# A phase's first two down weights split ahead of its last evacuation, and the last pair's silu queued behind them on ScalarE

## The chip, the cores and the metric

The kernel runs on one core of one Trainium2 chip. The time is device microseconds of one execution; the lower the better. A core has TensorE (matmuls, and the loads of their stationary operands, which the profile lists as PEld), VectorE (DVE), ScalarE (ACT), GpSimd (POOL) and SyncE (SP, used here to issue transfers). Each engine works through its own queue in order; semaphores connect them.

## The reference, cut to what matters

One layer of a hybrid encoder on 512 tokens of width 1024, in float32. The change lies in the last part, the channel mixer with its gated convolution:

```
h = rms_norm(x, norm_ffn_g)
up = causal_dwconv(h @ w_up, conv_ffn_w)     # 1024 -> 2 x 2816, three taps along the tokens
a, b = split(up, 2)
x = x + (silu(a) * b) @ w_down               # 2816 -> 1024
out = rms_norm(x, norm_f_g)
```

## The kernel before, in words

**Precision.** Every float32 operand of a matmul is split into a rounded half `h` and a remainder `l`, and a product is three matmuls: wh·xh, wl·xh and wh·xl. For a weight this is the work of `split()`: ScalarE copies the raw weight into `wh` (line 274), VectorE subtracts it to get `wl` (line 278). Both tiles have two buffers, so a weight can be split only once TensorE has finished with the weight two before it in the stream.

**Stream.** All weights stand in one list, `stream`, in the order in which they are used; `raws` counts those being loaded, `parts` those already split. `split()` also issues the raw loads some places ahead, on SP's queue.

**Phases.** The 22 pairs (a, b) of 128 hidden columns are done in two phases, pairs 0 to 11 and 12 to 21. In a phase the up products of its pairs come first: `up()` runs two blocks of matmuls per pair (`p_up`, one for a and one for b), and evacuates each: VectorE multiplies the sums by the norm factor (`fz`, line 1155), `taps` applies the three-tap convolution (ScalarE line 565, VectorE lines 566 and 569, result `fu`). After the second block `glu()` forms silu(a) on ScalarE (line 1215) and a·b: on GpSimd for most pairs, for a phase's last pair on VectorE and later (line 1232). Two pairs make a quadrant q, from which `glu` derives the forms that the fast matrix product needs: sums and differences (`t13`, `t24`, lines 1237 to 1242) and their halves `gh`, `gl` (`hl`, lines 1246 and 1247).

Then come the phase's down steps, in `seven()`: a fast product of 2 × 2 blocks with seven multiplications, whose weights come in two chunks per step, named P (three forms) and F (four forms). The first step of phase 0 uses P18 and F18, that of phase 1 P30 and F30. `seven()` takes a chunk, runs its matmuls (`passes`, line 326; for each chunk first all matmuls with `wh`, then those with `wl`), and then splits the next chunk by `split_next()` if that has not been done. In phase 1 the chunks are P30, F30, P31, F31 and so on; quadrant 10, of the last two pairs, is first needed by P33, in the fourth step. In phase 0 quadrant 5, of its last two pairs, is first needed by the fifth step.

**Order.** Where work is not to run at once, it is put into the list `later` as (due chunk, cost in us, tags, function). After each split `run_later` runs what is due within a budget that depends on the kind of chunk (for an F 0.75, for a P 1.6, for an up weight 1.7, or 4.2 while entries tagged `("e",)` wait). `flush` and `flush_only` run entries with given tags at once. The tag `("e",)` marks the evacuation of the pairs 1, 2 and 5, whose up products are also done by `seven()` (`merge`), and of up blocks evacuated while such entries still wait. Everything run from `later` is traced under `after_split()`, so on ScalarE it is queued behind the last `wh` traced so far, and on VectorE behind the last `wl`. `glu()` sets the due chunks of its follow-up work from the number of chunks split at that moment (k = len(parts) − 1): for a phase's last pair the product at k + 3, the sums at k + 4, the halves at k + 5 and k + 6. It also runs at once what is left of earlier quadrants.

Outside these rules the framework's scheduler orders each engine's queue from the order of tracing and from what it takes to be ready.

**The place of the change.** In `up()`, for the last pair of a phase (j = 11 and j = 21) and its second block (i = 1), after the block's matmuls are traced, `split_next()` splits the first P chunk. If entries tagged `("e",)` wait, they are flushed and one more chunk is split. Then the block is evacuated and `glu()` is called.

Of the kernel before, what the change touches and what calls it, by code (L numbers as in the profile page):

```python
# [10 lines left out]
AF = mybir.ActivationFunctionType  # L11
# [31 lines left out]
PHASES = ((0, 12), (12, NP))  # L43
# [27 lines left out]
def block_kernel(ctx, tc, xT, vecs, wv, win, wmix, wo, wup, wst, wdp, outT):  # L71
# [3 lines left out]
    nc = tc.nc  # L75
# [6 lines left out]
    def keep(ins):  # L82
        return tc.keep_in_program_order(ins)
# [70 lines left out]
    raws, parts, order = [], [], {}  # L154
    pools = {"raw": wp}
    later = []
    held = dict.fromkeys(NRAW, 0)

    def after_split():

        st = ExitStack()
        for ins in order.values():
            st.enter_context(tc.issue_after(ins))
        return st

    def tag_of(k):
        return "raw" if stream[k][0][0] != "F" else "rf" if k >= ff0 else "rg"

    def load(upto):
        for k in range(len(raws), min(upto, len(stream) - 1) + 1):  # L170
            nm, src, ncol = stream[k]
            tag = tag_of(k)
            if held[tag] == NRAW[tag] or tag not in pools:
                return
            held[tag] += 1
            raw = pools[tag].tile([P, D], F32, tag=tag, name=f"raw_{nm}", bufs=NRAW[tag])
            if k == 0:

                keep(nc.scalar.dma_start(raw[:, VB:ncol], src[:, VB:]))
                keep(nc.sync.dma_start(raw[:, :VB], src[:, :VB]))  # L180
            else:
                keep(nc.sync.dma_start(raw[:, :ncol], src if tag == "raw" else made[src]))
            raws.append(raw[:, :ncol])
# [39 lines left out]
    def run_later(k, us):  # L223

        n = 0
        while n < len(later):
            if later[n][0] <= k and later[n][1] <= us + 0.1:
                us -= later[n][1]
                with after_split():
                    later.pop(n)[3]()  # L230
            elif later[n][0] <= k:
                return
            else:
                n += 1
# [11 lines left out]
    def flush_only(tags):  # L246

        while n := [n for n, w in enumerate(later) if set(w[2]) & set(tags)]:
            with after_split():
                later.pop(n[0])[3]()  # L250

    def split(hl=None):

        k = len(parts)
        if k == len(stream):
            return
        nm, _, ncol = stream[k]
        load(k + (LOOK if len(raws) > KB else AHEAD))
        if hl is None:
            hl = []  # L260
            for x in "hl":
                if k == 0:
                    wp.tile([P, PADW[x]], F32, tag=f"pad{x}", name=f"pad_{x}")
                w0 = VOFF if k < KB else 0
                hl.append(wp.tile([P, D], F32R, tag=f"w{x}", name=f"w{x}_{nm}", bufs=2)[:, w0 : w0 + ncol])
        hi, lo = hl
        raw = raws[k]
        if k == 0:
            for cs in (slice(VB, S + H), slice(0, VB)):
                keep(nc.vector.tensor_copy(hi[:, cs], raw[:, cs]))  # L270
        elif k == 1:
            keep(nc.vector.tensor_copy(hi, raw))
        else:
            ins = nc.scalar.activation(hi, raw, AF.Copy)  # L274
            order["hi"] = ins.ins
            if k < KB:
                keep(ins)
        ins = nc.vector.tensor_sub(lo, raw, hi.bitcast(F32))  # L278
        order["lo"] = ins.ins
        if k < KB:  # L280
            keep(ins)
        held[tag_of(k)] -= 1
        parts.append((hi, lo))
        if any(("e",) in w[2] for w in later):
            run_later(k, {"u": 4.2, "P": 1.6, "F": 1.2}[nm[0]])
            return
        run_later(k, {"u": 1.7, "P": 1.6, "F": 0.75, "i": 3.0, "m": 3.0, "d": 0 if nm == "dp1" else 2.1}.get(nm[0], 3.5))
# [275 lines left out]
    def taps(u, z, w):  # L563

        nc.scalar.activation(u, z, AF.Copy, scale=col(w + 2))
        nc.vector.scalar_tensor_tensor(  # L566
            u[:, 1:], z[:, : S - 1], col(w + 1), u[:, 1:], op0=ALU.mult, op1=ALU.add
        )
        nc.vector.scalar_tensor_tensor(  # L569
            u[:, 2:], z[:, : S - 2], col(w), u[:, 2:], op0=ALU.mult, op1=ALU.add  # L570
        )
# [117 lines left out]
    z, e, o = (ap.tile([n, S], F32, tag="pp", name=nm, bufs=NPP) for nm in ("fz", "fe", "fo"))  # L689
# [104 lines left out]
    for i in range(n + LA):  # L794
# [8 lines left out]
        if 0 <= i - LA < n:  # L803
            pr, e, qb = units[i - LA]
# [151 lines left out]
    for j in range(KB):  # L956
# [26 lines left out]
        a, b = gs  # L983
# [141 lines left out]
    def up(j, ph, rb2, pu=None):  # L1125
        uu = []

        def tap(i, z):
            u = fp.tile([P, S], F32, tag="fu", name=f"fu{j}{i}", bufs=3)
            taps(u, z, CF + 3 * (2 * j + i))  # L1130
            uu.append(u)

        if j in SUP:
            c = len(GATES) + 2 * SUP.index(j)
            slot()
            seven(
                UPD[c - len(GATES) :][:2], c, {j: USETS[j]}, up_form, of="x",
                done=lambda i, banks, ids: merge(ph, j, banks, ids, rb2, tap, uu),
            )
            slot()  # L1140
            return
        evacs = []
        for i in range(2):
            slot()
            p = pu[i] if pu else block(f"up{2 * j + i}", x1h, x1l, True)
            if i and j + 1 == PHASES[ph][1]:
                split_next()
                if any(("e",) in w[2] for w in later):
                    flush_only((("e",),))
                    split()  # L1150
            z = [None]

            def mul(i=i, p=p, z=z):
                z[0] = fp.tile([P, S], F32, tag="fz", name=f"fz{j}{i}", bufs=4)
                nc.vector.tensor_mul(z[0], p, rb2)

            evac = [(0.7, mul), (1.4, lambda i=i, z=z: tap(i, z[0]))]
            if i:
                evac.append((0, lambda: glu(ph, j, uu)))
            if any(("e",) in w[2] for w in later):  # L1160
                later.extend((0, us, (("e",), acc.last) if x == 0 else (("e",),), f) for x, (us, f) in enumerate(evac))
            else:
                for _, f in evac:
                    f()
# [46 lines left out]
    def glu(ph, j, uu):  # L1211
        a, b = uu
        q, k = j // 2, len(parts) - 1
        g0 = place(ph, q)
        nc.scalar.activation(a, a, AF.Silu)
        if j == NP - 1:
            nc.scalar.activation(tbl, a[: 4 * H, :1], AF.Sqrt, scale=0.0, bias=eps[: 4 * H])
        if j % 2 == 0:
            ge = glu.even = fp.tile([P, 2, 2 * P], F32, tag="ge", name=f"ge{q}", bufs=2)
            keep(nc.gpsimd.tensor_mul(ge, a.rearrange(halves_of, h=2), b.rearrange(halves_of, h=2)))  # L1220
            return
        flush_only([("q", x) for x in range(q)])
        ge = glu.even
        go = fp.tile([P, 6, 2 * P], F32, tag="gr", name=f"go{q}")

        def mul(eng):
            return eng.tensor_mul(go[:, 0:2, :], a.rearrange(halves_of, h=2), b.rearrange(halves_of, h=2))

        if j + 1 < PHASES[ph][1]:
            keep(mul(nc.gpsimd))  # L1230
        else:
            later.append((k + 3, 0.7, (("q", q),), lambda: mul(nc.vector)))
        b11, b12 = ge[:, 0, :], ge[:, 1, :]
        b21, b22, t1, t2, t3, t4 = (go[:, i, :] for i in range(6))

        def t13():
            nc.vector.tensor_sub(t1, b11, b12)
            nc.vector.tensor_sub(t3, b22, b12)

        def t24():  # L1240
            nc.vector.scalar_tensor_tensor(t2, t1, -1.0, b22, op0=ALU.mult, op1=ALU.subtract)
            nc.vector.scalar_tensor_tensor(t4, t2, -1.0, b21, op0=ALU.mult, op1=ALU.subtract)

        def hl(src, gs):
            def f():
                nc.scalar.activation(gh[:, gs, :], src, AF.Copy)
                nc.vector.tensor_sub(gl[:, gs, :], src, gh.bitcast(F32)[:, gs, :])

            return f


        d = (2, 3, 4) if j + 1 < PHASES[ph][1] else (4, 5, 6)
        w = [(d[0], 0.85, t13), (d[0], 0.85, t24), (d[1], 0.7, hl(ge[:, : 1 + ph, :], slice(g0, g0 + 1 + NF * ph, NF)))]
        w += [(d[x > 0 and 2 or 1], 0.7, hl(go[:, x : x + 2, :], slice(g0 + 1 + x, g0 + 3 + x))) for x in (0, 4, 2)]
        at = next((x for x, i in enumerate(later) if ("e",) in i[2]), len(later))
        later[at:at] = [(k + n, us, (("q", q),), f) for n, us, f in w]
# [265 lines left out]
```

## Time and profile before

| | us |
|---|---|
| median of 3 runs | 695.1 |
| lowest and highest | 694.63, 695.14 |
| profiled execution, its own time | 695.06 |
| its span, first to last instruction | 693.2 |
| TensorE busy | 685.2 |
| VectorE busy | 537.2 |
| ScalarE busy | 359.9 |
| GpSimd busy | 178.5 |

The mean granted clock of TensorE is 0.997 of full speed. Phase 0's down steps begin near 466 us of the span, phase 1's near 633 us. In a timeline row the columns are start (us from the start of the span), duration in us, engine, line of the kernel, operation, output and inputs by name, shapes, and, in brackets, how long the engine had been idle before it and what released it. In a row of a stretch the columns are its bounds, its length, then the busy time and the number of instructions of TensorE, of the weight loads, of VectorE, ScalarE and GpSimd, then the granted clock, the share of the transfer engines that was busy, and GB/s.

### The profile page before, as it was taken

To read this page: it belongs to the slowest core of one execution; us is meant where nothing else is said; L and a number is where in the kernel's file an instruction comes from. 1 tells how busy PE (TensorE), PEld (TensorE's weight loads), DVE (VectorE), ACT (ScalarE), POOL (GpSimd) and SP (SyncE) were. 2 spreads that over 40 slices of the span, in tenths; PEclk is the share of its full clock that TensorE was granted. 3 is DMA by queue.
4 is the path that set the end of the run, shared out by engine and by line. 5 is a ranking of instruction groups with operands and counts; after the bars stand their busy time and mean duration, and the time that the engine had idled before them with its cause. 6 is when DMAs were issued, how large, how long until landed. Compare 5 with 4: busy or idle time off the path is not lost.

```text
span 693.2 us, 14638 instructions
## 1 busy us (share of the span) xinstructions
PE 685.2 (99%) x5960; PEld 683.7 (99%) x5960; DVE 537.2 (77%) x833; ACT 359.9 (52%) x568; POOL 178.5 (26%) x195
## 2 busy tenths in 40 slices
PE   9999999999999999999999999999999999999996
PEld 9999999999999999999999999999999999999996
DVE  6677887877578778869778699998774677877794
ACT  5575755555554444446554555545443344445572
POOL 6124947542020201214400143320000313222000
PEclk9999999999999999999999999999999999999998
DMA  8628999553568586787887486585647686766513
GB/s 311 218 66 290 217 238 213 132 124 92 183 145 220 165 272 200 232 306 158 126 279 240 125 190 175 143 219 193 192 132 227 143 194 159 185 171 178 156 31 122
DMA packets 60019, 127.57 MB, mean 184 GB/s; under 512 B 5376, under 2 KB 27920, under 8 KB 59696
## 3 DMA queue, kind: packets, MB, share of 16 engines
q1 hardware_dynamic: 41880, 101.51, 44.5%
q0 software_dynamic: 16832, 23.93, 22.0%
q10 hardware_dynamic: 1240, 1.19, 0.5%
q8 instruction: 47, 0.77, 0.5%
q14 instruction: 20, 0.16, 0.1%
HBM read 124.45 MB, written 41.42 MB: 239 GB/s over the span
## 4 chain that ended last, share of the span: by engine, by line
PE 89%; DVE 9%; issue 1%; ACT 1%; DVEq 0%; ACTq 0%
PE dn L326 25%; PE p_up L308 16%; PE p_in L308 14%; PE p_wo L308 6%; PE p_up L326 5%; PE yc L308 3%; PE ya L308 3%; DVE wl_up L278 2%; DVE fu L566 2%; PE pa L476 2%; PE pb L478 2%; PE p_q L308 2%; PE p_k L308 2%; PE o L657 2%; PE tp L640 1%; DVE fu L569 1%
## 5 line engine op out<-in xcount | busy, mean ns | idle before, releaser
L308 PE MATMUL p_up<-x1h,wh_up 128*128 128x256 f32 x464 | 90.4, 276 | 0.0
L308 PE MATMUL p_up<-x1h,wl_up 128*128 128x256 f32 x464 | 90.4, 276 | 0.0
L308 PE MATMUL p_up<-x1l,wh_up 128*128 128x256 f32 x464 | 90.3, 276 | 0.0
L210 POOL DMA_DIRECT2D f<-in_wst_dram x60 | 70.9, 1316 | 0.3 <-issue 0.2
L308 PEld LDWEIGHTS p_up<-x1h,wl_up 128*128 128x128 f32 x464 | 69.9, 188 | 0.0
L308 PEld LDWEIGHTS p_up<-x1l,wh_up 128*128 128x128 f32 x464 | 69.8, 188 | 0.0
L308 PEld LDWEIGHTS p_up<-x1h,wh_up 128*128 128x128 f32 x464 | 69.8, 188 | 0.0
L274 ACT ACTIVATE wh_up<-raw_up 128x1024 fp32r<-128x1024 f32 x38 | 40.2, 1057 | 53.4 <-PE p_up L308 42.9
L278 DVE TENSOR_TENSOR wl_F<-raw_F,wh_F 128x1024 fp32r<-128x1024 f32 (+1 forms) x38 | 51.0, 1343 | 17.9 <-ACT wh_F L274 17.9
L274 ACT ACTIVATE wh_F<-raw_F 128x1024 fp32r<-128x1024 f32 (+1 forms) x38 | 40.0, 1053 | 35.9 <-PE dn L326 27.2
L278 DVE TENSOR_TENSOR wl_up<-raw_up,wh_up 128x1024 fp32r<-128x1024 f32 x38 | 48.7, 1282 | 12.0 <-ACT wh_up L274 12.0
L308 PE MATMUL p_in<-xgh,wh_in 128*128 128x256 f32 x288 | 56.8, 279 | 0.0
L308 PE MATMUL p_in<-xgh,wl_in 128*128 128x256 f32 x288 | 56.6, 278 | 0.0
L308 PE MATMUL p_in<-xgl,wh_in 128*128 128x256 f32 x288 | 56.5, 278 | 0.0
L1220 POOL TENSOR_TENSOR ge<-fu,fu 128x512 f32<-128x512 f32 x11 | 16.7, 1520 | 146.9 <-DVE fu L569 116.1
L274 ACT ACTIVATE wh_P<-raw_P 128x768 fp32r<-128x768 f32 (+1 forms) x38 | 31.7, 834 | 32.9 <-PE dn L326 23.8
L278 DVE TENSOR_TENSOR wl_P<-raw_P,wh_P 128x768 fp32r<-128x768 f32 (+1 forms) x38 | 36.6, 962 | 15.4 <-ACT wh_P L274 9.5
L326 PE MATMUL dn<-gh,wh_F 128*128 128x256 f32 x192 | 45.2, 277 | 0.7 <-ACT wh_F L274 0.7
L308 PEld LDWEIGHTS p_in<-xgh,wh_in 128*128 128x128 f32 x288 | 44.7, 188 | 0.7
L326 PE MATMUL dn<-gl,wh_F 128*128 128x256 f32 x192 | 45.1, 276 | 0.0
L308 PEld LDWEIGHTS p_in<-xgl,wh_in 128*128 128x128 f32 x288 | 43.7, 188 | 0.0
L308 PEld LDWEIGHTS p_in<-xgh,wl_in 128*128 128x128 f32 x288 | 43.6, 188 | 0.0
(343 smaller groups left out, 2150.7 us busy)
## 6 DMA issues: line engine op xcount, KB each, us to landing
raw_up<-in_wup_dram SPq DMA_DIRECT2D x38, 512.0 KB, 5.1
raw_F<-f SPq DMA_DIRECT2D x37, 512.0 KB, 5.3
raw_P<-in_wst_dram SPq DMA_DIRECT2D x37, 384.0 KB, 4.8
raw_in<-in_win_dram SPq DMA_DIRECT2D x24, 512.0 KB, 3.8
f<-in_wst_dram POOLq DMA_DIRECT2D x37, 256.0 KB, 6.4
f<-in_wst_dram SPq DMA_DIRECT2D x18, 512.0 KB, 7.0
f<-in_wst_dram POOLq DMA_DIRECT2D x18, 512.0 KB, 7.8
f<-f SPq DMA_DIRECT2D x36, 256.0 KB, 6.2
```

The costliest lines, as they stand in the source:

```text
L210: return lambda: keep(nc.gpsimd.dma_start(dst, src, accum_op=ALU.add))
L274: ins = nc.scalar.activation(hi, raw, AF.Copy)
L278: ins = nc.vector.tensor_sub(lo, raw, hi.bitcast(F32))
L308: keep(nc.tensor.matmul(out[:, cs], w, x[:, cs], start=start and i == 0 and c == 0, stop=stop and i == 2 and c == len(cut) - 1,))
L326: keep(nc.tensor.matmul(out, wl if x == 1 else wh, xl if x == 2 else xh, start=opens and bk not in seen, stop=closes and bk not in left,))
L476: keep(nc.tensor.matmul(pa[t][:, :VW], xt, w[:, VB:], start=start, stop=stop))
L478: keep(nc.tensor.matmul(pb[t], xt, w[:, :VB], start=start and t % 2 == 0, stop=stop and t % 2 == 1))
L566: nc.vector.scalar_tensor_tensor(u[:, 1:], z[:, : S - 1], col(w + 1), u[:, 1:], op0=ALU.mult, op1=ALU.add)
L569: nc.vector.scalar_tensor_tensor(u[:, 2:], z[:, : S - 2], col(w), u[:, 2:], op0=ALU.mult, op1=ALU.add)
L640: keep(nc.tensor.transpose(tp[:, ks], pt[:, ks], ident))
L657: keep(nc.tensor.matmul(o[:, 2 * P * e + c0 : 2 * P * (e + 1)], w, x[:, kb, c0:], start=e == 0 and kb == 0 and i == 0, stop=e == 1 and kb ...
L1220: keep(nc.gpsimd.tensor_mul(ge, a.rearrange(halves_of, h=2), b.rearrange(halves_of, h=2)))
```

## The change

Two places change. In `up()`, at the end of a phase, the second `split()` no longer depends on whether entries tagged `("e",)` wait: the phase's first P chunk and its first F chunk are both split there, and only then are such entries flushed. In `glu()`, for the last pair of a phase, the silu is traced under `issue_after(order["hi"])`, which queues it on ScalarE behind the last `wh` traced so far, here that of the F chunk.

```diff
@@ -1145,9 +1145,8 @@
             p = pu[i] if pu else block(f"up{2 * j + i}", x1h, x1l, True)
             if i and j + 1 == PHASES[ph][1]:
                 split_next()
-                if any(("e",) in w[2] for w in later):
-                    flush_only((("e",),))
-                    split()
+                split()
+                flush_only((("e",),))
             z = [None]
 
             def mul(i=i, p=p, z=z):
@@ -1212,7 +1211,8 @@
         a, b = uu
         q, k = j // 2, len(parts) - 1
         g0 = place(ph, q)
-        nc.scalar.activation(a, a, AF.Silu)
+        with tc.issue_after(order["hi"]) if j + 1 == PHASES[ph][1] else ExitStack():
+            nc.scalar.activation(a, a, AF.Silu)
         if j == NP - 1:
             nc.scalar.activation(tbl, a[: 4 * H, :1], AF.Sqrt, scale=0.0, bias=eps[: 4 * H])
         if j % 2 == 0:
```

## The prediction

> **What bounds the kernel now.** I read the page first, then the waits of the TensorE, then the stretches of the span, and last the timeline at the two places that the diff touches.
>
> ```profile
> span 693.2 us, 14638 instructions
> PE 685.2 (99%) x5960; PEld 683.7 (99%) x5960; DVE 537.2 (77%) x833; ACT 359.9 (52%) x568; POOL 178.5 (26%) x195
> ```
> ```profile
> PE warm L115 <- DVE ones L107: 1.1, 1, 1.1
> PE dn L326 <- ACT wh_F L274: 0.7, 1, 0.7
> ```
> ```profile
> 397.00:465.00 68.00, 68.00 (x602) 68.00 (x602) 65.63 (x94) 34.89 (x52) 23.71 (x19) 1.00 0.72 186
> 465.00:524.00 59.00, 58.34 (x514) 58.15 (x514) 45.70 (x63) 28.96 (x37) 0.00 (x0) 1.00 0.59 181
> 627.00:669.00 42.00, 42.00 (x370) 41.81 (x370) 34.00 (x49) 24.91 (x34) 3.18 (x3) 1.00 0.46 132
> ```
>
> The matmuls fill the span. TensorE waits for another engine twice, once at the start (the `warm` row) and once, 0.7 us, for a `wh_F`, the rounded half of a down weight made by ScalarE. In the stretches (length, then busy time of PE, weight loads, VectorE, ScalarE, GpSimd, then granted clock) only 465 to 524, where phase 0 goes from up blocks to down steps, has idle PE; the clock is 1.00 in all three. VectorE is 97% busy (65.63 of 68) just before. So this edit can win only that one hole, and can lose by opening others. Phase 0's first down weights are P18 and F18, phase 1's P30 and F30.
>
> ```profile
> 464.01 0.94 DVE L278 TENSOR_TENSOR wl_P<-raw_P,wh_P 128x768 fp32r<-128x768 f32 x1
> 464.12 0.72 ACT L565 ACTIVATE fu<-fz,vec 128x512 f32<-128x512 f32 x1 [2.13 <-DVE fz L1155]
> 464.75 1.66 ACT L1246 ACTIVATE gh<-go 128x512 fp32r<-128x512 f32 x3
> 465.85 0.39 PE L308 MATMUL p_up<-x1l,wh_up 128*128 128x256 f32 x2
> 466.47 0.74 DVE L569 SCALAR_TENSOR_TENSOR fu<-fz,vec,fu 128x510 f32<-128x510 f32 x1
> 467.13 1.28 DVE L1247 TENSOR_TENSOR gl<-go,gh 128x512 fp32r<-128x512 f32 x2
> 467.30 0.63 ACT L1215 ACTIVATE fu<-fu 128x512 f32<-128x512 f32 x1 [0.90 <-DVE fu L569]
> 467.32 0.76 PEld L326 LDWEIGHTS dn<-gh,wl_P 128*128 128x128 f32 x6
> 467.84 1.04 ACT L274 ACTIVATE wh_F<-raw_F 128x1024 fp32r<-128x1024 f32 x1
> 468.33 0.68 DVE L1155 TENSOR_TENSOR fz<-p_up,rb_n 128x512 f32<-128x512 f32 x1
> 468.93 0.19 PEld L326 LDWEIGHTS dn<-gh,wh_F 128*128 128x128 f32 x1 [0.85 <-ACT wh_F L274]
> 469.04 0.19 PEld L326 LDWEIGHTS dn<-gl,wh_F 128*128 128x128 f32 x1
> 470.73 0.94 DVE L278 TENSOR_TENSOR wl_P<-raw_P,wh_P 128x768 fp32r<-128x768 f32 x1
> 471.67 0.19 PEld L326 LDWEIGHTS dn<-gh,wh_P 128*128 128x128 f32 x1
> 473.03 0.75 PEld L326 LDWEIGHTS dn<-gh,wl_P 128*128 128x128 f32 x6
> ```
> The reader sees ScalarE stand for 0.90 us until the last pair's first tap chain (`fu` L569) is done, then take its silu (L1215), and only then `wh_F`. P18's lower-half loads begin at 467.32, F18's first load at 468.93.
>
> ```profile
> 631.08 0.63 ACT L1215 ACTIVATE fu<-fu 128x512 f32<-128x512 f32 x1 [1.92 <-DVE fu L569]
> 631.73 1.28 ACT L1217 ACT_TABLE_LOAD   x1
> 632.71 0.39 PE L308 MATMUL p_up<-x1l,wh_up 128*128 128x256 f32 x2
> 633.02 0.29 ACT L1217 ACTIVATE tbl<-fu,ex 32x1 f32<-32x1 f32 x1
> 633.14 0.69 DVE L1155 TENSOR_TENSOR fz<-p_up,rb_n 128x512 f32<-128x512 f32 x1 [2.15 <-PE p_up L308]
> 633.23 1.04 ACT L274 ACTIVATE wh_F<-raw_F 128x1024 fp32r<-128x1024 f32 x1
> 634.18 0.71 ACT L565 ACTIVATE fu<-fz,vec 128x512 f32<-128x512 f32 x1
> 634.19 0.76 PEld L326 LDWEIGHTS dn<-gh,wl_P 128*128 128x128 f32 x6
> 634.79 0.83 ACT L274 ACTIVATE wh_P<-raw_P 128x768 fp32r<-128x768 f32 x1
> 634.87 0.19 PEld L326 LDWEIGHTS dn<-gh,wh_F 128*128 128x128 f32 x1
> 634.98 0.19 PEld L326 LDWEIGHTS dn<-gl,wh_F 128*128 128x128 f32 x1
> 637.59 0.19 PEld L326 LDWEIGHTS dn<-gh,wh_P 128*128 128x128 f32 x1
> ```
> At the end of phase 1 the same hand-over has no hole: silu, the load of the square-root table and its one small use lie in a ScalarE gap before the up weights' buffer is free.
>
> **The change, part by part.**
> *What really moves.* No instruction is added or taken away; order and due times change. The `("e",)` entries come only from pairs 1, 2 and 5; after pair 5 an up split may spend 4.2 and an evacuation adds 2.1 (the code's own units), so the queue of 6.9 is empty four splits on, long before pair 11, and phase 1 makes none. The moved `flush_only` thus finds nothing, and the old branch, second split included, never ran. New is: F18 and F30 are split, unconditionally, before the last product is evacuated; the silu is queued behind their `wh_F`; and as `glu` counts from the number of split chunks, the last quadrant's follow-up work falls due one chunk later.
>
> *Phase 0, the gain.* `wh_F` reuses the buffer of the last up weight, whose last matmul runs to 465.85 + 0.39 = 466.24, so this is its earliest start; it would end at 467.28. F18's load is wanted one undisturbed step after 467.32. Phase 1 gives that step: from the `wl_P` group to the second F load, 634.98 − 634.19 = 0.79. Here it is 469.04 − 467.32 = 1.72. The hole is worth 0.93 us, more than the 0.7 or 0.85 of the wait rows, because the restart is slow too. With `wh_F` ready at 467.28 against a need at about 468.0, all of it should go: −0.93. From below: 0, if `wh_F` still starts late. I take the full value since ScalarE is free at 464.75 + 1.66 = 466.41 and nothing ahead of `wh_F` then waits.
>
> *Phase 0, what hides the displaced work.* The silu goes from 467.30 to about 467.9 at the earliest; its product is due several chunks on. The two last `gh`/`gl` parts of quadrant 4, which `glu` flushes, get behind F18's halves as well. VectorE holds the same instructions. At 467.2 it has `fz` (its matmul ended at 466.24) or `wl_F` ready, so it need not stand. The next deadline is the second down step's `wl_P`: done at 470.73 + 0.94 = 471.67, needed at 473.03, which comes 0.93 earlier, at 472.10. Cover: 0.43 us. Cost 0; if VectorE stands for longer than 0.43, the excess goes to TensorE.
>
> *Phase 1, the loss.* `wh_F` cannot start before 632.71 + 0.39 = 633.10. Silu, table load and small use leave the gap and stand behind it. ScalarE then runs: `wh_F` from 633.14 (starts 0.95 apart by 633.23 and 634.18), `fu` from 634.09 (0.61 on, by 634.18 and 634.79), silu 634.70 (0.65), table load 635.35 (1.29), small use 636.64 (0.21 to 0.29), second step's `wh_P` from 636.85 to 637.70. Its first load is wanted at 637.59 and starts some 0.05 after the half is made (468.93 against 467.84 + 1.04 in phase 0): a stall of about 0.16, with a slow restart 0.2. Bounds: 0 if the scheduler puts `wh_P` in front, 0.5 if the small use and the restart take twice as long. I take 0.2, which the row sum gives.
>
> [...]
>
> *Phase 1, due times.* Quadrant 10 is consumed in the fourth down step.
> ```profile
> 641.69 0.42 DVE L1241 SCALAR_TENSOR_TENSOR go<-go 128x256 f32<-128x256 f32 x1
> 642.14 0.42 DVE L1242 SCALAR_TENSOR_TENSOR go<-go 128x256 f32<-128x256 f32 x1
> 643.99 0.68 DVE L1247 TENSOR_TENSOR gl<-ge,gh 128x512 fp32r<-128x512 f32 x1
> 644.90 0.96 DVE L278 TENSOR_TENSOR wl_P<-raw_P,wh_P 128x768 fp32r<-128x768 f32 x1 [0.22 <-ACT wh_P L274]
> 645.77 1.89 DVE L1247 TENSOR_TENSOR gl<-go,gh 128x512 fp32r<-128x512 f32 x3
> ```
> ```profile
> 647.22 0.28 PE L326 MATMUL dn<-gh,wh_P 128*128 128x256 f32 x1
> ```
> One chunk later, the split budgets (0.75 for an F, 1.6 for a P) leave the second pair of sums (641.69 to 642.56, 0.87) and the `ge` part (0.6) behind the `wl_P` of 644.90 instead of ahead of it. The three `go` parts then start at 645.77 + 0.87 + 0.6 = 647.24 instead of 645.77; the second, the last this step needs, ends at about 648.50. TensorE reaches it as its twelfth matmul, 647.22 + 11 × 0.114 = 648.47. So the margin is gone: 0.05. Bounds: 0, and 1.2 if the next `wl_F` gets in between. Quadrant 5 in phase 0 has the same lateness with a step more before it is used; cost 0.
>
> *DMA and queues.* `load` runs inside the split, so SP's next raw loads are issued in the same order; each waits for the raw buffer that the `wl` before it frees. GpSimd has nothing in 465 to 524, and nothing of its queue moves. No wait of TensorE names a DMA.
>
> *Sum.* The profiled execution took 695.06 (span 693.2, and 1.86 outside); the median of the runs shown is 695.1, 0.04 above. 695.06 − 0.93 + 0.2 + 0.05 = 694.38, so 694.4.
>
> **Rivals.**
> *The hole only moves (695.2).* ScalarE or VectorE reaches the second step late by what F18 gained: the 0.43 of cover is passed by about 0.9. For it: VectorE's 97% before the hand-over. Against it: the instructions are the same, and one of two is always ready. 694.4 + 0.9 = 695.3; with `wh_F` not earlier at all, 695.06 + 0.25 = 695.3; I give 695.2.
>
> *Slower: VectorE stands at `wl_F`.* If the scheduler queues `wl_F` straight behind the `wl_P` of 464.01, VectorE has nothing to run from 464.95 until `wh_F` is made at 467.28: 2.33 us, of which 1.9 pass the cover. 694.4 + 1.9 = 696.3. From 2.5 us of such standing on it decides: 0.2% of 695.06 is 1.39, which is also about what a measurement of this kernel can tell from no change; with some of the bound of the fourth step it comes to 696.7. Against it: the old order also had `wl_F` behind everything ready, and in phase 1 `fz` went first. [...]
>
> *Faster by more than 1.39.* TensorE has no other hole to close from 397 to 669, so nothing in the trace pays for it: 693.6 at best.
>
> **How the numbers follow.** Forecast (most of 0.93 gained, 0 to 0.6 given back) 0.62, its own range 693.9 to 695.0; hole moved 0.22, at 695.2; VectorE standing 0.12, of which 0.10 lies past 695.06 + 1.39 = 696.45 and 0.02 short of it; more gain 0.04. So faster by over 0.2% has 0.04, slower 0.10, and within 0.2% 0.62 + 0.22 + 0.02 = 0.86. The low end, 693.7, is the whole gain against the fastest run shown, 694.63 − 0.93; the high end, 695.9, takes in the moved hole, the upper bound of the second step's stall, and the near part of the slower case. Left out is about 0.15.
>
> **What would show it.** Right: at about 465 to 470 the PE wait for `wh_F` is gone, silu starts after `wh_F`, and the `wl_P` group and second F load stand 0.8 apart. Phase 1: table load after `wh_F` near 635, a short PE wait for `wh_P` near 637.6 less the gain, the `gl` parts of quadrant 10 behind the fourth step's `wl_P`. Wrong if VectorE shows an idle stretch before `wl_F`, or if TensorE shows a wait of a microsecond at the second or fourth step.

## The result, and the profile after

The changed kernel takes 696.1 us (median of 20 runs, 695.69 to 696.61), the kernel before 695.05 (20 runs, 694.56 to 696.16). The ratio is 1.0015, with a 95% interval of 1.0008 to 1.0022: slower by about 1 us, where 0.7 us less was forecast. The time lies 0.2 above the stated range.

The waits of TensorE, in the changed kernel:

```profile
PE dn L326 <- DVE gl L1247: 1.4, 1, 1.4
PE warm L115 <- DVE ones L107: 1.1, 1, 1.1
```

The same work is in it, from its page:

```profile
PE 685.5 (99%) x5960; PEld 683.9 (99%) x5960; DVE 537.4 (77%) x833; ACT 359.6 (52%) x568; POOL 178.6 (26%) x195
```

The wait for `wh_F` is gone, and one twice as long stands in another place, on another engine. The stretches of the changed kernel tell where (bounds, length, busy time of PE, weight loads, VectorE, ScalarE, GpSimd):

```profile
465.00:524.00 59.00, 58.97 (x520) 58.77 (x520) 45.69 (x64) 29.24 (x37) 0.00 (x0) 1.00 0.58 184
627.00:669.00 42.00, 40.64 (x356) 40.38 (x355) 32.82 (x47) 23.97 (x33) 2.46 (x3) 1.00 0.45 127
```

The hand-over of phase 0 has 58.97 us of matmuls in 59 (58.34 before); the down steps of phase 1 have 40.64 in 42 (42.00 before). First phase 0, from the timeline of the changed kernel:

```profile
466.22 1.06 ACT L274 ACTIVATE wh_F<-raw_F 128x1024 fp32r<-128x1024 f32 x1 [0.96 <-ACT gh L1246]
467.22 0.75 PEld L326 LDWEIGHTS dn<-gh,wl_P 128*128 128x128 f32 x6
468.01 0.19 PEld L326 LDWEIGHTS dn<-gl,wh_F 128*128 128x128 f32 x1
468.43 0.62 ACT L1215 ACTIVATE fu<-fu 128x512 f32<-128x512 f32 x1
470.63 0.73 DVE L569 SCALAR_TENSOR_TENSOR fu<-fz,vec,fu 128x510 f32<-128x510 f32 x1
471.29 0.94 DVE L278 TENSOR_TENSOR wl_P<-raw_P,wh_P 128x768 fp32r<-128x768 f32 x1
472.29 0.77 PEld L326 LDWEIGHTS dn<-gh,wl_P 128*128 128x128 f32 x6 [0.23 <-DVE wl_P L278]
```

`wh_F` starts at 466.22, the silu comes after it, and P18's `wl_P` group and the second F18 load stand 468.01 − 467.22 = 0.79 apart, as in an undisturbed step: the whole 0.93 is won. Of it about 0.3 is lost again at once, since the second step's `wl_P` is late (the weight loads stand 0.23 for it). From the first step's `wl_P` loads to the second's it was 473.03 − 467.32 = 5.71 before and is 472.29 − 467.22 = 5.07 now: a net gain of 0.64.

Then phase 1, at the fourth step (P33). The queues of VectorE and ScalarE and TensorE's last `wh` matmul of the step, in the changed kernel:

```profile
644.18 0.96 DVE L278 TENSOR_TENSOR wl_P<-raw_P,wh_P 128x768 fp32r<-128x768 f32 x1 [0.15 <-ACT wh_P L274]
645.06 0.42 DVE L1241 SCALAR_TENSOR_TENSOR go<-go 128x256 f32<-128x256 f32 x1
645.39 0.68 DVE L1247 TENSOR_TENSOR gl<-ge,gh 128x512 fp32r<-128x512 f32 x1
646.00 0.42 DVE L1242 SCALAR_TENSOR_TENSOR go<-go 128x256 f32<-128x256 f32 x1
646.33 1.29 DVE L1247 TENSOR_TENSOR gl<-go,gh 128x512 fp32r<-128x512 f32 x2
647.53 1.22 DVE L278 TENSOR_TENSOR wl_F<-raw_F,wh_F 128x1024 fp32r<-128x1024 f32 x1
648.67 0.69 DVE L1247 TENSOR_TENSOR gl<-go,gh 128x512 fp32r<-128x512 f32 x1
```
```profile
645.51 0.63 ACT L1246 ACTIVATE gh<-go 128x512 fp32r<-128x512 f32 x1 [0.32 <-DVE go L1241]
646.05 1.05 ACT L274 ACTIVATE wh_F<-raw_F 128x1024 fp32r<-128x1024 f32 x1
647.00 0.61 ACT L1246 ACTIVATE gh<-go 128x512 fp32r<-128x512 f32 x1
```
```profile
647.67 0.39 PE L326 MATMUL dn<-gh,wh_P 128*128 128x256 f32 x1
649.41 0.39 PE L326 MATMUL dn<-gl,wh_P 128*128 128x256 f32 x1 [1.36 <-DVE gl L1247]
```

Quadrant 10's three pairs of halves ran in one piece before (the row `gl` x3 of the prediction, ahead of the next `wl_F`). On ScalarE it was the same; from the kernel before:

```profile
644.77 1.66 ACT L1246 ACTIVATE gh<-go 128x512 fp32r<-128x512 f32 x3
646.51 1.07 ACT L274 ACTIVATE wh_F<-raw_F 128x1024 fp32r<-128x1024 f32 x1
```

Now only two do; then both engines turn to the next F weight, and the third pair comes behind it: `gh` at 647.00 behind `wh_F`, `gl` at 648.67 behind `wl_F`. TensorE stands at the twelfth matmul of P33 until that `gl` ends at 649.36.

Two landmarks, points of TensorE's work that both traces have, measure the loss: the `wl` groups of the first P and of the fourth F step of phase 1. Before:

```profile
634.30 0.84 PE L326 MATMUL dn<-gh,wl_P 128*128 128x256 f32 x6
...
651.07 1.07 PE L326 MATMUL dn<-gh,wl_F 128*128 128x256 f32 x8
```
After:
```profile
633.58 0.84 PE L326 MATMUL dn<-gh,wl_P 128*128 128x256 f32 x6
...
652.17 1.07 PE L326 MATMUL dn<-gh,wl_F 128*128 128x256 f32 x8
```

16.77 us became 18.59: a loss of 1.82. Together −0.64 + 1.82 = +1.18; the span grew by 1.0 (694.2 against 693.2), the profiled execution by 1.03 (696.09 against 695.06). Some 0.1 of the rest lies ahead of P18, which TensorE reached 0.10 earlier; the last section shows how such a difference comes without any edit.

### The profile page after: what moved, and what is told of

Its sections match the earlier page's. It is cut to its first block, busy times and chain, and to the rows that moved or that the text cites. A ratio compares the mean times of both kernels' runs of the same rounds, so it can differ in the third digit from the quotient of the medians.

```text
span 694.2 us, 14636 instructions
## 1 busy us (share of the span) xinstructions
PE 685.5 (99%) x5960; PEld 683.9 (99%) x5960; DVE 537.4 (77%) x833; ACT 359.6 (52%) x568; POOL 178.6 (26%) x195
```

## The experiments

Two theories could explain the loss. The **due-time theory**: phase 1 loses because `glu` counts chunks, so that one chunk split early makes the last quadrant's follow-up work fall due one chunk later. The **ScalarE theory**: phase 1 loses because `wh_F` of F30, the silu and the table load have changed places, which pushes ScalarE's and VectorE's work of the phase back. The runs undo one at a time.

**Due chunks put back (e1_due_back).**
```diff
 # against the changed kernel
-        q, k = j // 2, len(parts) - 1
+        q, k = j // 2, len(parts) - 1 - (j + 1 == PHASES[ph][1])
```


> The changed kernel, but the last pair's follow-up work falls due at the chunks of the kernel before (one chunk earlier than in the changed kernel); both early splits and the held silu stay. Due-time theory: the 1.80 us that TensorE loses in the fourth step of phase 1 come only from the follow-up work being one chunk late, so that loss goes, phase 0's gain of 0.72 stays, and the time is 695.05 - 0.72 = 694.3. ScalarE theory: the loss comes from the early F30 split with silu and table load behind it, which push ScalarE's and VectorE's work of phase 1 back, so the loss stays and the time is 696.1.

Measured: 694.46 (11 runs), ratio to before 0.9992 (0.9983 to 1.0000). The list of waits of TensorE's matmuls has only the one at the start, and the landmarks of phase 1 stand 650.13 − 633.35 = 16.78 apart, as before the change. From the timeline of this run:

```profile
633.35 0.84 PE L326 MATMUL dn<-gh,wl_P 128*128 128x256 f32 x6
...
650.13 1.07 PE L326 MATMUL dn<-gh,wl_F 128*128 128x256 f32 x8
```

The early split of F30, the held silu and the moved table load are all still in it, so they cost nothing between these landmarks. The ScalarE theory falls.

**Due chunks alone (e5_due_only).**
```diff
 # against the kernel before
-        q, k = j // 2, len(parts) - 1
+        q, k = j // 2, len(parts) - 1 + (j + 1 == PHASES[ph][1])
```


> The kernel before, with nothing but the due chunks of the last pair's follow-up work moved one later, in both phases; no early split, no held silu. Due-time theory: phase 0 keeps its hole, the fourth step of phase 1 loses 1.8, the time is 695.05 + 1.8 = 696.9, and TensorE waits there for a gl half of quadrant 10. ScalarE theory: no loss, 695.05.

Measured: 696.75 (11 runs), ratio 1.0023 (1.0013 to 1.0033). TensorE's waits in this run:

```profile
PE dn L326 <- DVE gl L1247: 1.4, 1, 1.4
PE warm L115 <- DVE ones L107: 1.1, 1, 1.1
PE dn L326 <- ACT wh_F L274: 0.7, 1, 0.7
PE pa L476 <- DVE wh_v L272: 0.3, 1, 0.3
```

Both waits are there: the old one, since nothing was split early, and the new one, to the tenth. The `pa` row lies in the first 9 us of the span, far ahead of the edit; it stands in some of the profiles and not in others. No weight was split earlier and no silu held. The loss is the due time's.

**Early split in one phase alone (e3_split_ph0, e4_split_ph1).**
```diff
 # against the changed kernel (ph == 1 in the second)
-                split()
+                if ph == 0:
+                    split()
```


> The changed kernel with the early second split in phase 0 alone; in phase 1 only the P chunk is split early and the silu stands behind that chunk's half, so phase 1's due times are those of before. Both theories: phase 0 gains 0.72, phase 1 loses nothing, 694.3. If phase 0's gain is paid back somewhere later, 695.0.

> The changed kernel with the early second split in phase 1 alone, due times shifted there as in the changed kernel. Both theories: phase 0 keeps its hole of 0.93 and the fourth step of phase 1 loses 1.80, so 695.05 + 1.8 = 696.9. If the two places are not independent, the sum of this run's and the phase 0 run's differences will not be the changed kernel's +1.05.

Measured: phase 0 alone 694.11 (11 runs), ratio 0.9990 (0.9981 to 0.9998); phase 1 alone 697.0 (9 runs), ratio 1.0027 (1.0017 to 1.0037). The differences to the kernel before, 694.91 in these runs, are −0.80 and +2.09. Their sum, +1.29, is the changed kernel's +1.05 within what the intervals allow (each is some 0.6 either way). The traces say it more sharply. In the run with phase 0 alone the first two `wl_P` loads of phase 0 stand 5.07 apart, as in the changed kernel, and the landmarks of phase 1 stand 16.77 apart, as in the kernel before. In the run with phase 1 alone it is 5.70, as before, and 18.59, as in the changed kernel. So each place does the same with or without the other. Both runs hold the silu in both phases: in the second, phase 0 has the hold without the early split and still waits 0.7 us for `wh_F`, so the hold alone gains nothing.

**The second pair of sums ahead again, all else late (e7_t24_free).**
```diff
 # against the changed kernel
-        w = [(d[0], 0.85, t13), (d[0], 0.85, t24), ...
+        w = [(d[0], 0.85, t13), (d[0], 0.85 if j + 1 < PHASES[ph][1] else 0, t24), ...
```


> The changed kernel, both early splits, the hold and the late due chunks kept; only the cost that the list books for the second pair of sums of a phase's last quadrant is 0 instead of 0.85, so that they run after the F32 split, together with the first pair, instead of after the P33 split. If the fourth step's loss comes from the last gh/gl halves of quadrant 10 waiting for these sums and so getting behind the next F weight's split on ScalarE and VectorE, it goes with them: 694.3. If being one chunk late costs by itself, whatever the order of the sums, most of the 1.8 stays: 695.7 to 696.1.

Measured: 694.6 (11 runs), ratio 0.9991 (0.9982 to 1.0000). VectorE in the fourth step of this run:

```profile
643.78 0.42 DVE L1241 SCALAR_TENSOR_TENSOR go<-go 128x256 f32<-128x256 f32 x1
644.12 0.95 DVE L278 TENSOR_TENSOR wl_P<-raw_P,wh_P 128x768 fp32r<-128x768 f32 x1
644.99 0.42 DVE L1242 SCALAR_TENSOR_TENSOR go<-go 128x256 f32<-128x256 f32 x1
645.32 0.69 DVE L1247 TENSOR_TENSOR gl<-ge,gh 128x512 fp32r<-128x512 f32 x1
645.92 1.89 DVE L1247 TENSOR_TENSOR gl<-go,gh 128x512 fp32r<-128x512 f32 x3
647.73 1.22 DVE L278 TENSOR_TENSOR wl_F<-raw_F,wh_F 128x1024 fp32r<-128x1024 f32 x1
```

L1241 now runs ahead of the step's `wl_P` and L1242 right behind it, ahead of the `ge` half (in the changed kernel behind it); the three `go` halves stay together ahead of `wl_F`, and TensorE does not wait. So it is not lateness as such: the follow-up work is still due a chunk late. It is that the sums came so late that a pair of halves lost its place to the next weight. The run moves both sums; that L1242 is the one that counts is read from the rows of the changed kernel, where the `gh` made from it runs at 647.00, behind `wh_F`, while the pair behind L1241 kept its place.

**The early split without the hold (e9_ph0_nohold).**
```diff
 # against the kernel with the early split in phase 0 alone
-        with tc.issue_after(order["hi"]) if j + 1 == PHASES[ph][1] else ExitStack():
-            nc.scalar.activation(a, a, AF.Silu)
+        nc.scalar.activation(a, a, AF.Silu)
```


> Early second split in phase 0 alone, and the silu not held. If the hold makes the gain, ScalarE takes the silu first again as soon as its tap chain is done (near 467.1 in the span), F18's rounded half comes after it, TensorE waits for it again some 0.7 us, and the time is 694.9 to 695.05. If the early split alone makes the gain, the time is that of the run with early split in phase 0 and hold, 694.1.

Measured: 695.38 (11 runs), ratio 1.0005 (0.9996 to 1.0013): the gain is gone. From its timeline:

```profile
466.91 0.63 ACT L1215 ACTIVATE fu<-fu 128x512 f32<-128x512 f32 x1 [1.94 <-DVE fu L569]
467.45 1.04 ACT L274 ACTIVATE wh_F<-raw_F 128x1024 fp32r<-128x1024 f32 x1
468.52 1.23 DVE L278 TENSOR_TENSOR wl_F<-raw_F,wh_F 128x1024 fp32r<-128x1024 f32 x1 [1.10 <-ACT wh_F L274]
468.54 0.19 PEld L326 LDWEIGHTS dn<-gh,wh_F 128*128 128x128 f32 x1 [0.86 <-ACT wh_F L274]
473.19 0.77 PEld L326 LDWEIGHTS dn<-gh,wl_P 128*128 128x128 f32 x6 [0.50 <-DVE wl_P L278]
```

ScalarE stands 1.94 us for the silu's input, then takes the silu, then `wh_F`: the old hole of 0.86. VectorE, which now has `wl_F` queued ahead of the rest, stands 1.10 us too, and TensorE's weight loads stand 0.50 for the second step's `wl_P`. From the first step's `wl_P` loads (466.92) to the second's it is 473.19 − 466.92 = 6.27 against 5.71 in the kernel before: in the trace the early split without the hold loses 0.56, which the times can neither confirm nor exclude. The hold is what moves `wh_F` forward.

**Quadrant 4's last halves ahead of the split (e8_ph0_flush_q4).**
```diff
 # against the kernel with the early split in phase 0 alone
                 if ph == 0:
+                    flush_only([("q", 4)])
                     split()
```


> Early second split in phase 0 alone, with the hold, and the two last gh/gl halves of quadrant 4 run ahead of that split instead of behind it. In the run without this TensorE still waits 0.24 us for the second step's wl_P. If that wait comes from these halves lying between wl_F and wl_P on VectorE, it goes and the time is 693.8; if VectorE simply has too much to do there, the wait stays and the time is 694.1.

Measured: 694.54 (11 runs), ratio 0.9988 (0.9979 to 0.9996), not to be told from the run without this edit. The wait only moved, from the second step's `wl_P` to the first step's `wl_F`:

```profile
470.38 1.01 PEld L326 LDWEIGHTS dn<-gh,wl_F 128*128 128x128 f32 x8 [0.32 <-DVE wl_F L278]
```

Neither answer fits. In both orders VectorE works without a break up to the late weight, so in each order it has too much to do ahead of that weight. But behind it, in this run, VectorE stands 0.32 us for the next `wh_P`, so it is not shown that the work of the whole stretch is too much. Whether a third order avoids the wait was not tried.

**The better version once more (e12_best).** The same code as the early split in phase 0 alone.

> The kernel with the early second split in phase 0 alone, with the hold, once more, to see whether its lead holds: TensorE gains 0.62 between the first and the second down step of phase 0 and loses nothing in phase 1, so 0.6 to 0.8 us below the kernel before (ratio 0.9990), 694.3. If the first run's lead was chance, ratio 1.0000.

Measured: 694.38 (11 runs) against 695.06, ratio 0.9989 (0.9980 to 0.9998). Its landmarks stand 5.07 and 16.77 apart again. With 694.11 against 694.91 in the first run, this version is 0.7 to 0.8 us faster than the kernel before (the intervals reach from 0.1 to 1.4); against the changed kernel it was not timed side by side.

## Why the prediction was wrong, point by point

- *What bounds the kernel:* right. TensorE fills the span, and each term could be read as a hole in its work.
- *What really moves:* right. The counts of instructions of all five rows are those of before, and the effect is one of order and due times alone.
- *Phase 0, the gain of 0.93:* right in size and place (0.79 between the two loads), and the hold was needed for it. The slow restart counted in it stands in the trace of the kernel before: 0.23 from F18's first matmul, at 468.93, to its second, at 469.16, where later ones stand 0.11 apart.
- *Phase 0, cost 0 within a cover of 0.43:* too kind. The working held VectorE's order fixed up to the second step's `wl_P`, which in the kernel before ran at 470.73, ahead of the last tap:

```profile
471.60 0.74 DVE L569 SCALAR_TENSOR_TENSOR fu<-fz,vec,fu 128x510 f32<-128x510 f32 x1
```

  In the changed kernel this tap ran at 470.63 and the `wl_P` behind it, at 471.29. The cover was passed: 0.93 won, 0.64 left. This is a third of the rival in which the hole only moves.
- *Phase 1, the loss of 0.2 at the second step:* the lower bound, 0, was the value; the scheduler put `wh_P` ahead of the table load:

```profile
634.05 0.62 ACT L1215 ACTIVATE fu<-fu 128x512 f32<-128x512 f32 x1
634.57 0.83 ACT L274 ACTIVATE wh_P<-raw_P 128x768 fp32r<-128x768 f32 x1
635.42 1.28 ACT L1217 ACT_TABLE_LOAD   x1
636.72 0.29 ACT L1217 ACTIVATE tbl<-fu,ex 32x1 f32<-32x1 f32 x1
```

  The load took 1.28, as in the kernel before, and the small use starts 0.02 after its end (635.42 + 1.28 = 636.70, the next start 636.72).
- *Phase 1, due times, 0.05:* this is the step that failed. The mechanism was named (sums and halves behind the fourth step's `wl_P`, no margin left), and the number taken was the end at which it just fits; it measured 1.82. The working put the three `go` halves in the order in which the code traces them, so that the pair needed was the second. The queue held them in the order in which their inputs came: L1242, which feeds the pair needed, ran behind the `ge` half, so that pair came third. Once it was third it was behind the next `wl_F` and `wh_F`. The bound of 1.2 named just this, but counted VectorE's `wl_F` alone; TensorE's stop at 649.41 in place of about 647.78 is 1.63, and of the remaining 0.19 the restart takes 0.12 (0.23 from 649.41 to the next matmul, at 649.64; in the kernel before 0.11 between the same two, 648.47 and 648.58). Even that bound would not have left the range: 695.06 − 0.93 + 0.2 + 1.2 = 695.53. What carried the time past it is that the loss was 1.82 (695.06 − 0.93 + 1.82 = 695.95), with the 0.3 of phase 0 on top. The sign named for being wrong, a wait of a microsecond at the fourth step, is what came.
- *Sum:* −0.93 + 0.3 + 0 + 1.82 = +1.2 against a profiled +1.03. The sum forecast was −0.68.
- *Rivals:* the slower one was put in the wrong place. VectorE did not stand at `wl_F` in phase 0: it ran `fz` first. The run without the hold shows that mechanism, with 1.10 us of standing and 0.56 lost. The slower case that came was the bound of a term priced at 0.05, which had no rival of its own and so almost no chance. The 1.39 us taken for what a measurement can tell from no change was too much: the interval of the result is about 0.5 us either way.

## What to carry to other kernels

A term whose margin is worked out as nothing (648.50 against 648.47 here) is not worth its midpoint: it is a step, whose other side was here a whole weight split on two engines (1.82 us), and it should stand as a rival with its own chance. When a planner's due times are counted from the state at tracing, moving a step ahead of the count shifts all that hangs on it: look for every reader of the count (`len(parts)`) before costing the step itself. A queue order must be worked out from when the inputs come, not from the order of the code alone.

## What had not been expected

Two profiles of the same code, e3_split_ph0 and e12_best, reach phase 0's first `wl_P` loads at different times, 467.09 and 467.42; over all kernels, which have the same work up to there, it was 466.92 to 467.49. The difference is made in the first 9 us of the span, where TensorE's first matmuls run slower than the later ones, 0.63 us a pair against 0.40, and the turn does not come at the same time. The same two matmuls in e3_split_ph0 and in e12_best:

```profile
6.28 0.40 PE L478 MATMUL pb<-wh_v,xgh 128*128 128x256 f32 x2
...
6.36 0.63 PE L478 MATMUL pb<-wh_v,xgh 128*128 128x256 f32 x2
```

A `pa` matmul (L476) a little later starts at 8.66 in the one and 8.99 in the other, 0.33 apart, and 0.33 it still is at 467. The kernel before and the changed kernel have such a turn too (a `pb` pair takes 0.63 at 5.50 in both, 0.40 at 7.05 and at 6.91), and their profiles give the granted clock there as 1.00; what sets the turn no run shows.

This is as large as some of the effects studied, so the terms above are distances within one trace, not differences of starts between two. The 0.72 of the expectations is such a difference (634.30 − 633.58) and takes in the 0.10 from ahead of P18. Distances are not exact either: from phase 0's first `wl_P` loads to phase 1's first `wl_P` matmuls the changed kernel has 166.36 and e3_split_ph0 166.34, but e12_best, with the code of the latter, 166.56.
